# Differential attention of a prompt: score matmuls over 64 rows, the two components by turns, keys in pieces of 256

## The chip, the cores and the metric

The kernel runs on one core of one Trainium2 chip. The metric is the device time of one execution in microseconds (us); before the change the median of three runs is 1026.13 us (1025.02 to 1028.12).

## The reference

One layer of a streaming encoder serves a prompt of 512 tokens and a sample of 64 tokens with 256 cached ones; the width is 1024. The layer is a mixer (half gated delta rule, "GDN", half differential attention), attention to a memory of 256 rows, and a feed-forward net. The change lies in the differential attention. It has 4 heads, each with two components of 64 channels, and the same values for both:

```python
# q, k: (batch, positions, 4 heads, 2 components, 64);  v: (batch, positions, 4 heads, 128)
s = einsum('bqhcd,bkhcd->bhcqk', q, k) * 64 ** -0.5
visible = k_pos[None, :] < ((q_pos // 64 + 1) * 64)[:, None]     # causal by chunks of 64
p = softmax(where(visible, s, -inf))
a = p[:, :, 0] - lam * p[:, :, 1]
o = einsum('bhqk,bkhe->bqhe', a, v)                               # then an RMS norm per head
```

The prompt attends to itself, the sample to its 256 cached keys and its own 64.

## The kernel before

Prompt and sample are one axis of T = 576 tokens, channels on the partitions. Weights are split in a high and a low part (`wh`, `wl`, fp32r), and `project` multiplies each 128 output channels in two halves of the tokens (256 and 320) into banks named `pr`. The program first turns and normalizes the input, projects the inputs of the GDN heads, runs the GDN chunks, and then for each of the four heads `h` calls `diff_project(h)` and `diff_head(h, ...)`. After the heads come the memory keys and values (weights as the moving operand), the output projection, the memory attention and the feed-forward net.

`diff_project` projects queries, keys and values of a head. A head's 128 query channels are component 0 (partitions 0 to 63) and component 1 (64 to 127). They are evacuated into a tile `qz` (two of them, taken by turns by the heads) that has a plane for each component, in which the other component's 64 partitions are zero: GpSimd clears them once, at the start. So a score matmul can take all 128 partitions of the keys (`kdT`, in the profile `u`; the cached keys `ckT` are another `u`) and gets one component's scores.

`diff_head` goes through five tiles of 128 queries: t = 4 (the last 64 prompt queries and the 64 of the sample, of which only the latter are used, against 256 + 64 keys), then t = 0 to 3 with 128, 256, 384 and 512 keys. For each component it writes the scores into a bank, `g0` or `g1` (both `g` in the profile; there is one of each), masks a corner (L976), takes the row's maximum on VectorE (L980), scales it (L981), and lets ScalarE write the exponentials into `p0` or `p1` (L983). The two are combined on VectorE (L985 to L988), turned by TensorE into a bank `ba` (L113, `tr`), copied to `aT`, and multiplied with the values into `gs`. All matmuls go through one helper at L107, so in the profile they are told apart by their tiles. GpSimd also clears the end of a short tile (L990).

The order of the work on each engine is not the order of the code: a scheduler places the instructions by dependency, priority and modelled times, so matmuls of one head's attention stand between those of the next head's projections.

Of the kernel before, what the change touches and what calls it, by code (L numbers as in the profile page):

```python
# [8 lines left out]
F32 = mybir.dt.float32  # L9
# [6 lines left out]
P = 128  # L16
D = 1024
KT = 8
SEQ = 512
DEC = 64  # L20
T = SEQ + DEC
HALVES = ((0, 256), (256, T - 256))
PAST = 256
# [14 lines left out]
def hybrid_layer_kernel(  # L38
# [10 lines left out]
    V, A, G = nc.vector, nc.scalar, nc.gpsimd  # L49
# [17 lines left out]
    cp = ctx.enter_context(tc.tile_pool(name="cp", bufs=1))  # L67
# [11 lines left out]
    def nm(s):  # L79
        uid[0] += 1  # L80
        return f"{s}_{uid[0]}"
# [18 lines left out]
    def bank(tag="ba"):  # L100
        return ps.tile([P, 512], F32, tag=tag, name=nm(tag), bufs=BANKS[tag])
# [4 lines left out]
    def mm(out, lhsT, rhs, start=True, stop=True, pin=False, skip_group_check=False):  # L106
        i = nc.tensor.matmul(out, lhsT, rhs, start=start, stop=stop, skip_group_check=skip_group_check)  # L107
        if pin:
            tc.keep_in_program_order(i)
# [83 lines left out]
    def add_to(dst, b, more):  # L193
        A.copy(dst, more)
        V.tensor_tensor(dst, b, dst, ALU.add)
# [39 lines left out]
    def turn(src, n, q, tag, by=None):  # L235

        b = bank(tag)
        for i in range(4):
            o, f = b[:, i * P : i * P + n], src[:n, (4 * q + i) * P : (4 * q + i + 1) * P]
            if by is None:  # L240
                tr(o, f)
            else:
                mm(o, f, by[:n, :n])
        return b.rearrange("p (i t) -> p i t", i=4)[:, :, :n]
# [230 lines left out]
    with tc.issue_after(behind_keys[1]):  # L475
        ones2, triu2 = const([P, P], "ones2"), const([P, P], "triu2")
        G.memset(ones2, 0.0)
        for i in range(2):
            R = slice(i * DEC, (i + 1) * DEC)
            G.memset(ones2[R, R], 1.0)  # L480
        G.tensor_tensor(triu2, triu, ones2, ALU.mult)
# [12 lines left out]
    for a0, n in HALVES:  # L494
        b = bank("pr")
# [7 lines left out]
    b = bank()  # L503
# [37 lines left out]
    def halves_of(dst, src):  # L541

        for i in range(2):
            R = slice(i * DEC, (i + 1) * DEC)
            V.tensor_copy(dst[R], src[R, 4, i::2])

# [24 lines left out]
    for j in range(3):  # L571
        b = bank()
# [14 lines left out]
    for bi in range(2):  # L587
        scale(mn[:, bi, :], mt[:, bi, :], root(squares(mn[:, bi, :], mt[:, bi, :], P), P), gkv, P)
        for q in range(2):
            src = turn(mn[:, bi, :], P, q, "ba")  # L590
# [178 lines left out]
    def normed(q, nb, parts, out):  # L769

        so, co = tiny([P, nb], "tg"), tiny([P, nb], "tg")
        for R, src in parts:
            A.activation(out[R], src, AF.Square)
        V.tensor_reduce(so, out, AX.X, ALU.add)
# [119 lines left out]
    od, kdT = e3[:, 0], e5[:, 0]  # L894
# [2 lines left out]
    cv2 = view(e3, 1, 4, 4 * P).rearrange("p (i b) n -> p i b n", i=2)  # L897
    ckT, cvv = cv2[:, 0].rearrange("p b (c n) -> p (b c) n", n=PAST), cv2[:, 1]

    qz = [cp.tile([P, 2, T], F32, tag=f"qz{i}", name=f"qz{i}") for i in range(2)]  # L900
    with tc.issue_after(behind_keys[0]), tc.issue_after(behind_keys[1]):
        for q2 in qz:
            G.memset(q2[64:, 0, :], 0.0)
            G.memset(q2[:64, 1, :], 0.0)
        G.memset(vs[64:], 0.0)

    def diff_project(h):
        hs = slice(h * P, (h + 1) * P)
        for kind, base in (("q", 2056), ("k", 2568), ("v", 3080)):
            def evac(b, a0, n, more):  # L910
                ts_ = slice(a0, a0 + n)
                if kind == "q":
                    for c in range(2):
                        R = slice(64 * c, 64 * c + 64)
                        if more is not None:
                            add_to(qz[h % 2][R, c, ts_], b[R], more[R])
                        else:
                            (A.copy if c else V.tensor_copy)(qz[h % 2][R, c, ts_], b[R])
                    return
                d = small("zr", [P, 320])[:, :n] if kind == "v" else kdT[:, h, ts_]  # L920
                if more is not None:
                    add_to(d, b, more)
                else:
                    V.tensor_copy(d, b)
                bt = bank()
                for t in range(2):
                    tr(bt[:, t * P : (t + 1) * P], d[:, t * P : (t + 1) * P])
                if a0:
                    tr(bt[:DEC, 256:384], d[:, 256:])
                src, t2 = bt[:, :256].rearrange("p (t d) -> p t d", t=2), slice(a0 // P, a0 // P + 2)  # L930
                if kind == "v":
                    A.copy(vtm[:, t2, hs], src)
                    if a0:
                        A.copy(vs[:DEC, h, :], bt[:DEC, 256:384])
                else:
                    ko = small("ko", [P, 3, P])
                    A.copy(ko[:, :2], src)
                    nc.sync.dma_start(o_dk_p[0, 0, a0 : a0 + 256, h, :].rearrange("(t p) d -> p t d", p=P), ko[:, :2])
                    if a0:
                        A.copy(ko[:DEC, 2], bt[:DEC, 256:384])  # L940
                        nc.sync.dma_start(o_dk_s[0, 0, :, h, :], ko[:DEC, 2])

            project(weights(w2, base + h * P), xs, evac)
        nc.sync.dma_start(o_dv_p[0, 0, :, h, :].rearrange("(t p) d -> p t d", p=P), vtm[:, :, hs])
        nc.sync.dma_start(o_dv_s[0, 0, :, h, :], vs[:DEC, h, :])
# [11 lines left out]
    def diff_head(h, between):  # L957


        hs = slice(h * P, (h + 1) * P)  # L960
        so, co = tiny([P, 5], "ta"), tiny([P, 5], "ta")
        on = small("an", [P, 5, P])
        for t in (4, 0, 1, 2, 3):
            if t == 1:
                between()
            q0 = QT[t][0]
            nk = q0 + P if t < 4 else PAST + DEC
            nb = (nk + P - 1) // P
            pr = []
            mx, l = tiny([P, 2], "ta"), tiny([P, 2], "ta")  # L970
            for c in range(2):
                b = bank(f"g{c}")
                qq = qz[h % 2][:, c, q0 : q0 + P]
                if t < 4:
                    mm(b[:, :nk], qq, kdT[:, h, :nk])
                    V.memset(b[:64, nk - 64 : nk], -1e30)  # L976
                else:
                    mm(b[:, :PAST], qq, ckT[:, h, :])
                    mm(b[:, PAST:nk], qq, kdT[:, h, SEQ:T])
                V.tensor_reduce(mx[:, c : c + 1], b[:, :nk], AX.X, ALU.max)  # L980
                V.tensor_scalar(mx[:, c : c + 1], mx[:, c : c + 1], -0.125, None, ALU.mult)  # L981
                p = small(f"p{c}", [P, 512])
                A.activation(p[:, :nk], b[:, :nk], AF.Exp, bias=mx[:, c : c + 1], scale=0.125, accum_out=l[:, c : c + 1])  # L983
                pr.append(p)
            V.reciprocal(l, l)  # L985
            V.tensor_tensor(l[:, 1:2], l[:, 1:2], nlam, ALU.mult)
            V.tensor_scalar(pr[1][:, :nk], pr[1][:, :nk], l[:, 1:2], None, ALU.mult)
            V.scalar_tensor_tensor(pr[0][:, :nk], pr[0][:, :nk], l[:, 0:1], pr[1][:, :nk], ALU.mult, ALU.add)  # L988
            if nk < nb * P:
                G.memset(pr[0][:, nk : nb * P], 0.0)  # L990
            bt = bank()
            aT = small("aT", [P, 4, P])
            for kb in range(nb):
                tr(bt[:, kb * P : (kb + 1) * P], pr[0][:, kb * P : (kb + 1) * P])
            A.copy(aT[:, :nb, :], v4(bt, nb))
            po = bank("gs")[:, :P]
            for kb in range(nb):
                if t < 4:
                    vv = vtm[:, kb, hs]
                else:  # L1000
                    vv = cvv[:, kb, hs] if kb < 2 else vs[:, h, :]
                mm(po, aT[:, kb, :], vv, start=kb == 0, stop=kb == nb - 1)
            A.activation(pr[1][:, :P], po, AF.Square, accum_out=so[:, t : t + 1])
            A.copy(on[:, t, :], po)

        def finish():
            V.tensor_scalar(so, so, 1.0 / P, EPS, ALU.mult, ALU.add)
            rpow(co, so)
            V.tensor_tensor(on, on, co.unsqueeze(2).to_broadcast([P, 5, P]), ALU.mult)
            b, b2 = bank(), bank()  # L1010
            for t in range(4):
                tr(b[:, t * P : (t + 1) * P], on[:, t, :])
            tr(b2[:, :P], on[:, 4, :])
            for src, ts_ in ((b, slice(0, SEQ)), (b2[:, DEC:P], slice(SEQ, T))):
                A.activation(od[:, h, ts_], src, AF.Identity, scale=dn)

        return finish
# [23 lines left out]
    for w, out in ((w_mem_k, o_mk), (w_mem_v, o_mv)):  # L1041
        dst = tokens
        for f in range(2):
            fs = slice(512 * f, 512 * f + 512)
            bs = [bank("pr") for _ in range(2)]
            for kc in range(4):
                wt = split_weights(w[0, 256 * kc : 256 * kc + 256, fs], [P, 2, 512])
                for k in (2 * kc, 2 * kc + 1):
                    for t in range(2):
                        ts_ = slice(t * P, (t + 1) * P)  # L1050
# [10 lines left out]
            if out is o_mk:  # L1061
                for i in range(2):
                    b = bank()
# [79 lines left out]
    for k2 in range(KT // 2):  # L1143
        b = bank()
# [6 lines left out]
    for h in range(H):  # L1151
# [15 lines left out]
        for t, (q0, _) in enumerate(QT):  # L1167
            t0, n = TT[t]
            kk, kl = (mkT, mkl) if t < 4 else (cmT, cml)
            b = bank(("gs", "g0", "g1")[t % 3])  # L1170
# [25 lines left out]
        for i in range(2):  # L1196
            b, b2 = bank(("g0", "gs")[i]), bank(("g1", "ba")[i])
# [335 lines left out]
    for m in range(KT):  # L1533
# [3 lines left out]
        if m in (3, 4):  # L1537
            t = m - 3
# [43 lines left out]
```

## Time and profile before

| | |
|---|---|
| median of three runs | 1026.13 us |
| the profiled execution, and its span | 1024.58 us, 1022.9 us |
| granted TensorE clock, mean | 0.995 |
| TensorE matmuls, busy | 1002.1 us (98%) |
| VectorE, ScalarE, GpSimd, busy | 703.3, 535.3, 57.1 us |
| score matmuls (`g<-u,qz`), first to last start | 279.7 to 377.0 us |

The page gives the span in shares by engine and the chain of work that ended last. A row of the group view reads: line, engine, operation, output tile <- input tiles, shape, count, then busy us, mean ns of one, and idle time before. For TensorE a form such as 64*128 is the rows and columns of the array that the instruction uses, and 64x256 the partitions and elements of an operand. A timeline row has start, duration, engine, line, tiles and the number of equal instructions merged. PEld is the load of a matmul's stationary operand, which normally runs under the matmul before. An fp32 matmul appears as two instructions, each with its load; an fp32r matmul as one.

### The profile page before, as it was taken

How to read it: one execution, taken by the hardware profiler on the slowest of the kernel's cores; microseconds unless marked ns; L12 is line 12 of the kernel's file. 1: busy time of each engine (PE TensorE's matmuls, PEld its weight loads, DVE VectorE, ACT ScalarE, POOL GpSimd, SP SyncE). 2: the span in 40 equal slices, each digit the busy share in tenths (PEclk: the TensorE clock that was granted, in tenths of full speed). 3: DMA queues.
4: the chain of work that ended last, by engine and by line, in shares of the span. 5: the costliest groups of instructions: out<-in, count | busy, mean ns of one | idle time of the engine just before them, and what ended most of it. 6: DMA issues, size and time to landing. Idle time of an engine off the chain costs nothing.

```text
span 1022.9 us, 17296 instructions
## 1 busy us (share of the span) xinstructions
PE 1002.1 (98%) x6630; PEld 921.1 (90%) x6630; DVE 703.3 (69%) x1529; ACT 535.3 (52%) x1170; POOL 57.1 (6%) x123
## 2 busy tenths in 40 slices
PE   9999999999999999999999999999999999999996
PEld 7989899998888877899999998999999999999986
DVE  6666785676567676665665886757766677777883
ACT  6654664443364665544454656655545554555434
POOL 3441010100000000000000000000000000000000
PEclk9999999999999999999999999999999999999999
DMA  7432320100312255624121233422222222222202
GB/s 210 124 109 68 103 90 22 44 21 22 104 47 81 74 190 185 186 83 125 44 60 42 64 113 93 125 83 83 83 83 84 83 83 83 83 83 86 80 1 93
DMA packets 121254, 89.99 MB, mean 88 GB/s; under 512 B 5506, under 2 KB 112128, under 8 KB 120660
## 3 DMA queue, kind: packets, MB, share of 16 engines
q1 hardware_dynamic: 120804, 88.24, 29.0%
q8 instruction: 52, 0.85, 0.3%
q10 hardware_dynamic: 368, 0.66, 0.2%
q14 instruction: 30, 0.25, 0.1%
HBM read 79.14 MB, written 9.74 MB: 87 GB/s over the span
## 4 chain that ended last, share of the span: by engine, by line
PE 84%; DVE 3%; issue 3%; ACT 2%; POOL 2%; DMA 1%; POOLq 0%; ACTq 0%; DVEq 0%; SPq 0%
PE pr L107 49%; PE g L107 14%; PE ba L107 10%; PE gs L107 7%; PE ba L113 2%; PE g L113 2%; DMA r<-in_w_ff_dram 1%; DVE wl L162 0%; POOL tg L208 0%; DVE p L457 0%; DMA out_dram<-S 0%; DMA S<-in_state_gdn_dram 0%; POOL X L604 0%; DVE on L780 0%; ACT L645 0%
## 5 line engine op out<-in xcount | busy, mean ns | idle before, releaser
L107 PE MATMUL pr<-u,wh 128*128 128x320 f32 (+2 forms) x1240 | 327.1, 342 | 1.0 <-DVE p L323 1.0
L107 PE MATMUL pr<-u,wl 128*128 128x256 f32 (+1 forms) x816 | 228.3, 304 | 0.0
L107 PEld LDWEIGHTS pr<-u,wh 128*128 128x128 f32 x1240 | 211.5, 188 | 17.1 <-DVE p L323 1.3
L107 PEld LDWEIGHTS pr<-u,wl 128*128 128x128 f32 x816 | 149.8, 189 | 3.5 <-issue 0.7
L162 DVE TENSOR_TENSOR wl<-raw,wh 128x1024 fp32r<-128x1024 f32 x65 | 79.5, 1223 | 43.4 <-ACT wh L161 41.6
L161 ACT CAST wh<-raw 128x1024 fp32r<-128x1024 f32 x65 | 68.2, 1049 | 72.6 <-PE pr L107 55.7
L107 PE MATMUL pr<-u,w2h 128*128 128x320 f32 (+1 forms) x384 | 99.3, 343 | 2.8 <-DVE u L1415 2.8
L1330 ACT CAST w2h<-r 128x512 fp32r<-128x512 f32 x56 | 34.7, 620 | 92.6 <-PE pr L107 89.5
L107 PE MATMUL pr<-f,w2h 128*128 128x320 f32 (+1 forms) x288 | 73.8, 340 | 0.0
L107 PEld LDWEIGHTS pr<-u,w2h 128*128 128x128 f32 x384 | 65.7, 190 | 8.1 <-DVE u L1415 3.1
L107 PE MATMUL pr<-u,w2l 128*128 128x256 f32 (+1 forms) x256 | 65.7, 298 | 0.0
L107 PE MATMUL ba<-u,wl 128*128 128x288 f32 x360 | 54.0, 300 | 2.1 <-ACT keep L1366 2.0
L1415 DVE TENSOR_TENSOR u<-u,pr 128x256 f32<-128x256 f32 x96 | 43.0, 450 | 18.6 <-PE pr L107 18.0
L107 PEld LDWEIGHTS ba<-u,wl 128*128 128x128 f32 x360 | 50.4, 192 | 2.7 <-ACT keep L1366 2.7
L107 PEld LDWEIGHTS pr<-f,w2h 128*128 128x128 f32 x288 | 48.7, 188 | 4.1 <-issue 1.2
L107 PEld LDWEIGHTS pr<-u,w2l 128*128 128x128 f32 x256 | 47.7, 192 | 1.6
L107 PE MATMUL pr<-f,w2l 128*128 128x256 f32 (+1 forms) x192 | 48.8, 295 | 0.0
L1331 DVE TENSOR_TENSOR w2l<-r,w2h 128x512 fp32r<-128x512 f32 x56 | 38.5, 688 | 11.7 <-ACT w2h L1330 11.5
L208 POOL TENSOR_TENSOR tiny<-tiny,nhalf 128x1 f32<-128x1 f32 (+4 forms) x10 | 8.2, 822 | 629.6 <-DVE tiny L1479 537.9
L107 PE MATMUL pr<-wh,u 128*128 128x512 f32 x128 | 41.2, 401 | 0.0
L107 PEld LDWEIGHTS pr<-f,w2l 128*128 128x128 f32 x192 | 35.2, 188 | 1.1
L1375 ACT ACTIVATE c<-c 128x288 f32<-128x288 f32 x48 | 21.0, 442 | 28.6 <-DVE c L1374 28.6
(503 smaller groups left out, 2076.9 us busy)
## 6 DMA issues: line engine op xcount, KB each, us to landing
raw<-in_w_ff_dram SPq DMA_DIRECT2D x36, 512.0 KB
raw<-in_w_in_dram SPq DMA_DIRECT2D x28, 512.0 KB
r<-in_w_ff_dram SPq DMA_DIRECT2D x56, 256.0 KB
raw<-in_w_mem_k_dram SPq DMA_DIRECT2D x8, 512.0 KB
raw<-in_w_mem_v_dram SPq DMA_DIRECT2D x8, 512.0 KB
raw<-in_w_out_dram SPq DMA_DIRECT2D x8, 512.0 KB
raw<-in_w_mem_q_dram SPq DMA_DIRECT2D x8, 512.0 KB
raw<-in_w_mem_o_dram SPq DMA_DIRECT2D x8, 512.0 KB
```

Of the source, the lines that this page charges most:

```text
L107: i = nc.tensor.matmul(out, lhsT, rhs, start=start, stop=stop, skip_group_check=skip_group_check)
L113: i = nc.tensor.transpose(out, in_, ident[:n, :n])
L161: A.copy(wh, raw)
L162: V.tensor_tensor(wl, raw, wh.bitcast(F32), ALU.subtract)
L208: G.tensor_tensor(out, in_, bc(nhalf[: in_.shape[0], 0:1], list(in_.shape)), ALU.pow)
L1330: A.copy(wh, src)
L1331: V.tensor_tensor(wl, src, wh.bitcast(F32), ALU.subtract)
L1375: A.activation(c, c, AF.Relu)
L1415: V.tensor_tensor(am, am, b, ALU.add)
```

## The change

`qz` loses its second plane and its zeros: both components stand in one plane of 128 partitions, evacuated at full height, and the clearing on GpSimd goes. Each score matmul takes 64 partitions of queries and keys, 0 to 63 for component 0 and 64 to 127 for component 1. The keys are cut into pieces of at most 256, and the code issues for each piece first component 0, then component 1. What follows (mask, maximum, exponentials) is unchanged and starts when both components are issued. Per head 12 matmuls become 16.

```diff
--- before.py
+++ after.py
@@ -897,11 +897,8 @@
     cv2 = view(e3, 1, 4, 4 * P).rearrange("p (i b) n -> p i b n", i=2)
     ckT, cvv = cv2[:, 0].rearrange("p b (c n) -> p (b c) n", n=PAST), cv2[:, 1]
 
-    qz = [cp.tile([P, 2, T], F32, tag=f"qz{i}", name=f"qz{i}") for i in range(2)]
+    qz = [cp.tile([P, T], F32, tag=f"qz{i}", name=f"qz{i}") for i in range(2)]
     with tc.issue_after(behind_keys[0]), tc.issue_after(behind_keys[1]):
-        for q2 in qz:
-            G.memset(q2[64:, 0, :], 0.0)
-            G.memset(q2[:64, 1, :], 0.0)
         G.memset(vs[64:], 0.0)
 
     def diff_project(h):
@@ -910,12 +907,10 @@
             def evac(b, a0, n, more):
                 ts_ = slice(a0, a0 + n)
                 if kind == "q":
-                    for c in range(2):
-                        R = slice(64 * c, 64 * c + 64)
-                        if more is not None:
-                            add_to(qz[h % 2][R, c, ts_], b[R], more[R])
-                        else:
-                            (A.copy if c else V.tensor_copy)(qz[h % 2][R, c, ts_], b[R])
+                    if more is not None:
+                        add_to(qz[h % 2][:, ts_], b, more)
+                    else:
+                        V.tensor_copy(qz[h % 2][:, ts_], b)
                     return
                 d = small("zr", [P, 320])[:, :n] if kind == "v" else kdT[:, h, ts_]
                 if more is not None:
@@ -968,15 +963,17 @@
             nb = (nk + P - 1) // P
             pr = []
             mx, l = tiny([P, 2], "ta"), tiny([P, 2], "ta")
-            for c in range(2):
-                b = bank(f"g{c}")
-                qq = qz[h % 2][:, c, q0 : q0 + P]
+            sc = [bank(f"g{c}") for c in range(2)]
+            keys = [(kdT[:, h], k0, min(k0 + 256, nk), 0) for k0 in range(0, nk, 256)]
+            if t == 4:
+                keys = [(ckT[:, h], 0, PAST, 0), (kdT[:, h], PAST, nk, SEQ - PAST)]
+            for src, k0, k1, d in keys:
+                for c in range(2):
+                    R = slice(64 * c, 64 * c + 64)
+                    mm(sc[c][:, k0:k1], qz[h % 2][R, q0 : q0 + P], src[R, k0 + d : k1 + d])
+            for c, b in enumerate(sc):
                 if t < 4:
-                    mm(b[:, :nk], qq, kdT[:, h, :nk])
                     V.memset(b[:64, nk - 64 : nk], -1e30)
-                else:
-                    mm(b[:, :PAST], qq, ckT[:, h, :])
-                    mm(b[:, PAST:nk], qq, kdT[:, h, SEQ:T])
                 V.tensor_reduce(mx[:, c : c + 1], b[:, :nk], AX.X, ALU.max)
                 V.tensor_scalar(mx[:, c : c + 1], mx[:, c : c + 1], -0.125, None, ALU.mult)
                 p = small(f"p{c}", [P, 512])
```

The scheduler's order changes only from the first head's scores on as far as TensorE is concerned. The 64 score matmuls stand in it in 40 runs, each between other matmuls; 33 of the runs hold one component only. Three places on TensorE:

The first head's first prompt tile, 128 keys (`g0` is component 0, `g1` component 1, `pr` a projection). Before the change TensorE has here:

```order
L107 MATMUL pr_643_3450<-u_7_94,wl_642_3447 128x256
L107 MATMUL g0_527_2935<-u_4_78,qz0_2679 128x128
L107 MATMUL pr_643_3450<-u_7_94,wh_641_3446 128x512
L107 MATMUL g1_529_2942<-u_4_78,qz0_2679 128x128
L107 MATMUL pr_643_3450<-u_7_94,wl_642_3447 128x256
L107 MATMUL pr_643_3450<-u_7_94,wh_641_3446 128x512
L107 MATMUL pr_643_3450<-u_7_94,wl_642_3447 128x256 x2
L107 MATMUL pr_643_3450<-u_7_94,wh_641_3446 128x512
```

After it, at the same place of the program:

```order
L107 MATMUL pr_643_3448<-u_7_94,wl_642_3445 128x256
L107 MATMUL g0_527_2928<-u_4_78,qz0_2679 128x128
L107 MATMUL pr_643_3448<-u_7_94,wh_641_3444 128x512
L107 MATMUL pr_643_3448<-u_7_94,wl_642_3445 128x256
L107 MATMUL pr_643_3448<-u_7_94,wh_641_3444 128x512
L107 MATMUL pr_643_3448<-u_7_94,wl_642_3445 128x256 x2
L107 MATMUL pr_643_3448<-u_7_94,wh_641_3444 128x512
L107 MATMUL pr_644_3467<-u_6_93,wh_641_3444 128x320 x2
L107 MATMUL g1_528_2929<-u_4_78,qz0_2679 128x128
```

Before, one projection matmul stands between the two components; after, eight.

The second head's sample tile, 256 cached keys (`u_2_76`) and 64 of its own (`u_4_78`); `ba` is a transpose, `gs` the product with the values. Before the change:

```order
L107 MATMUL pr_651_3529<-u_6_93,wh_646_3500 128x320
L107 MATMUL g0_592_3265<-u_2_76,qz1_2680 128x256
L107 MATMUL gs_551_3017<-u_4_78,aT_550_3012 128x128 x3
L107 MATMUL g0_592_3265<-u_4_78,qz1_2680 128x64
L107 MATMUL g1_594_3272<-u_2_76,qz1_2680 128x256
L107 MATMUL g1_594_3272<-u_4_78,qz1_2680 128x64
L107 MATMUL pr_651_3529<-u_6_93,wh_646_3500 128x320
```

After it, at the same place of the program:

```order
L107 MATMUL g0_592_3259<-u_2_76,qz1_2680 128x256
L113 MATMUL ba_549_3006<-ident_79,p0_547_2995 128x128 x3
L107 MATMUL g0_592_3259<-u_4_78,qz1_2680 128x64
L107 MATMUL pr_651_3524<-u_6_93,wl_647_3496 128x320
L107 MATMUL pr_651_3524<-u_6_93,wh_646_3495 128x320 x2
L107 MATMUL pr_651_3524<-u_6_93,wl_647_3496 128x320
L107 MATMUL gs_551_3012<-u_4_78,aT_550_3007 128x128 x3
L107 MATMUL pr_651_3524<-u_7_94,wh_646_3495 128x320 x2
L107 MATMUL pr_651_3524<-u_7_94,wl_647_3496 128x320
L107 MATMUL pr_651_3524<-u_7_94,wh_646_3495 128x320 x2
L107 MATMUL g1_593_3260<-u_2_76,qz1_2680 128x256
L107 MATMUL g1_593_3260<-u_4_78,qz1_2680 128x64
```

Before, component 0 is cut once by other work and component 1 follows it; after, four score matmuls stand in three runs, no two components side by side.

The second head's tile of 512 keys, before the change:

```order
L107 MATMUL pr_717_3813<-u_7_94,wl_716_3810 128x256
L107 MATMUL g0_630_3400<-u_4_78,qz1_2680 128x512
L113 MATMUL ba_616_3356<-ident_79,p0_613_3343 128x128 x2
L107 MATMUL pr_717_3813<-u_7_94,wl_716_3810 128x256
L107 MATMUL pr_717_3813<-u_7_94,wh_715_3809 128x512
L107 MATMUL pr_718_3834<-u_6_93,wh_715_3809 128x320
L107 MATMUL gs_618_3361<-u_4_78,aT_617_3357 128x128 x2
L107 MATMUL pr_718_3834<-u_6_93,wh_715_3809 128x320
L107 MATMUL g1_632_3407<-u_4_78,qz1_2680 128x512
L107 MATMUL pr_718_3834<-u_6_93,wl_716_3810 128x320
```

After it, at the same place of the program:

```order
L107 MATMUL pr_718_3831<-u_7_94,wl_716_3809 128x320
L107 MATMUL pr_718_3831<-u_7_94,wh_715_3808 128x320 x2
L107 MATMUL g0_630_3396<-u_4_78,qz1_2680 128x256 x2
L107 MATMUL g1_631_3397<-u_4_78,qz1_2680 128x256 x2
L107 MATMUL pr_718_3831<-u_7_94,wl_716_3809 128x320
```

Before, each component is one matmul of 512 in a place of its own; after, two pieces of component 0 are followed by two of component 1, in one run.

## The prediction

> **What bounds it.** I read the page first, then TensorE's waits in the stretch where the four heads run, then the rows of the score matmuls, and last the few places where this kernel already puts matmuls of 64 rows between matmuls of 128.
>
> ```profile
> span 1022.9 us, 17296 instructions
> PE 1002.1 (98%) x6630; PEld 921.1 (90%) x6630; DVE 703.3 (69%) x1529; ACT 535.3 (52%) x1170; POOL 57.1 (6%) x123
> PE 84%; DVE 3%; issue 3%; ACT 2%; POOL 2%; DMA 1%; POOLq 0%; ACTq 0%; DVEq 0%; SPq 0%
> ```
>
> TensorE is busy for 98% of the span and carries 84% of the chain that ended last. A busy row alone is weak evidence, because the ends of pipelined matmuls are modelled, so I look at the stage itself. The score matmuls lie between 279.5 and 377.0 us. The windows view of the stretch around them, and the waits of TensorE from 140 us (where the first queries are evacuated) to 382 us, read:
>
> ```profile
> 276.00:382.00 106.00, 104.91 (x618) 87.33 (x617) 72.68 (x240) 63.28 (x209) 4.54 (x7) 1.00 0.32 102
> PE gs L107 <- DVE on L780: 2.1, 4, 0.9
> PE gs L107 <- DMA S<-in_state_gdn_dram: 0.3, 1, 0.3
> ```
>
> In 106 us the matmul row is busy 104.91, VectorE 72.68 and ScalarE 63.28, and in 242 us TensorE's matmuls waited for anybody only 2.4 us. While a head's softmax runs, the next head's projections fill TensorE. So in this stage time is what TensorE spends: what the change takes from its row comes off the end, what it adds goes on.
>
> **The score matmuls now.** By tile and form they are these (an fp32 matmul is two instructions in the trace, so 48 matmuls are 96 rows):
>
> ```profile
> L107 PE MATMUL g<-u,qz 128*128 128x256 f32 x32 | 9.1, 386 | 0.0
> L107 PE MATMUL g<-u,qz 128*128 128x512 f32 x16 | 8.6, 617 | 0.0
> L107 PE MATMUL g<-u,qz 128*128 128x384 f32 x16 | 6.9, 514 | 0.0
> L107 PE MATMUL g<-u,qz 128*128 128x128 f32 x16 | 3.5, 300 | 0.0
> L107 PE MATMUL g<-u,qz 128*128 128x64 f32 x16 | 2.6, 247 | 0.0
> 294.76 1.06 PE L107 MATMUL g<-u,qz 128*128 128x512 f32 x2
> 295.65 0.38 PE L113 MATMUL ba<-ident,p 128*128 128x128 f32 x2
> ```
>
> The mean durations contain the pipeline's latency; what counts is when the next one starts. Two of 512 columns start at 294.76 and the next work starts at 295.65: 0.89 us, or 0.87 ns per column of one instruction. All 96 stream 32x256 + 16x(512+384+128+64) = 25,600 columns, 22.3 us. That is the most that is at stake: perfect pairing would save half, 11.1 us.
>
> **What removes work.** Half the rows of the old operand were zeros; the new matmuls have 64 rows each but the same number of columns, so alone each holds the array as long as before. Time is saved only where a matmul of rows 0 to 63 and one of rows 64 to 127 stand next to each other, so that both can stream at once. The order shows how often that is. The code issues the components by turns, but the scheduler hands them out by its own priorities: the 64 matmuls stand in 40 separate runs, and only 7 runs hold both halves. An fp32 matmul is two passes, and the second pass of one half can meet only the first pass of the other. Over these 7 runs the meeting passes have 384+256+128+256+128+256+128 = 1,536 columns, 1.3 us at 0.87 ns. Bounds are 0 (they stream one after the other) and -1.3; no run here shows two halves streaming at once and none shows them refusing, the operands and the banks (g0, g1) are disjoint, and I take -1.3.
>
> **What adds work.** Every one of the 40 runs stands between matmuls of 128 rows, and the kernel shows already what such a change of row count costs. One place is a transpose of the 64 sample rows, the other a 64-row block of the triangular inverse. TensorE's timeline in three windows:
>
> ```profile
> 49.13 0.30 PE L107 MATMUL pr<-u,wl 128*128 128x320 f32 x1
> 49.37 0.46 PE L113 MATMUL g<-ident,u 64*128 64x64 f32 x4
> 49.76 0.56 PE L107 MATMUL pr<-u,wh 128*128 128x320 f32 x2
> 50.15 0.31 PE L107 MATMUL pr<-u,wl 128*128 128x320 f32 x1
> 50.29 0.46 PE L107 MATMUL pr<-u,wh 128*128 128x320 f32 x2
> ...
> 170.34 0.38 PE L107 MATMUL g<-Y,X 128*128 128x128 f32 x2
> 170.66 0.68 PE L107 MATMUL g<-X,Y 64*64 64x64 f32 x8
> 171.26 0.94 PE L107 MATMUL g<-Y,X 128*128 128x128 f32 x6
> ...
> 299.01 0.31 PE L107 MATMUL pr<-u,wh 128*128 128x320 f32 x1
> 299.16 0.61 PE L107 MATMUL g<-u,qz 128*128 128x256 f32 x2
> 299.60 0.83 PE L107 MATMUL gs<-u,aT 128*128 128x128 f32 x6
> ```
>
> First place: a 320-column fp32r matmul holds the array 0.14 (50.15 to 50.29), so the one at 49.13 is done streaming at 49.27. The next 128-row pair starts at 49.76 and takes 0.56 where the same pair takes 0.46 at 50.29, so it really streams from 49.86. Of these 0.59 us the four 64-column matmuls need 4x0.055 = 0.22 (eight take 0.22 longer than four: 0.68 against 0.46). The rest, 0.37, is the price of going in and out. Second place: two of 128 columns need 0.22, so they are done at 170.56; eight of 64 need 0.44; the next start at 171.26, and six of them take 0.94 where six take 0.83 at 299.60, so 0.11 more: 171.26 + 0.11 - 170.56 - 0.44 = 0.37. If the 64-column matmuls are paced at 0.06 instead of 0.055, the first reading gives 0.35 and the second 0.33. The third window is the score matmul as it stands now: 299.01 plus 0.14 is 299.15, it starts at 299.16, two of 256 columns take 0.44, which is their 512x0.87 = 0.445; no price at all. Where it comes from is seen in the weight loads:
>
> ```profile
> 48.98 0.19 PEld L107 LDWEIGHTS pr<-u,wl 128*128 128x128 f32 x1
> 49.36 0.32 PEld L113 LDWEIGHTS g<-ident,u 64*128 64x128 f32 x4 [0.19 <-ACT u L283]
> 49.75 0.30 PEld L107 LDWEIGHTS pr<-u,wh 128*128 128x128 f32 x2
> L107 PEld LDWEIGHTS g<-u,qz 128*128 128x128 f32 x96 | 15.6, 189 | 3.3 <-ACT p L983 1.2
> L113 PEld LDWEIGHTS g<-ident,u 64*128 64x128 f32 x12 | 1.0, 138 | 0.5 <-ACT u L283 0.5
> ```
>
> The weights of 49.13 were loaded at 48.98, under the matmul before. The load of the 64-row group starts only at 49.36, 0.09 after the array ran dry, and that of the next 128-row matmul at 49.75, when the group has drained too: on both sides the load is bare. I take 0.35 for a run in and out: 40 x 0.35 = +14.0 us. Bounds: 40 x 0.33 = 13.2 and 40 x 0.37 = 14.8; if a score run waited anyway for a bank or a query, part of its price would be hidden, which the 2.4 us of waits limit.
>
> The Trainium skill, "TensorEngine Tiling (Array Packing)", section Key Properties, says that changing the tiling mode, not just the tile, drains TensorE; the trace agrees, with about 0.09 us before each bare load, and this is the rule that speaks against the change. The Trainium skill, "TensorE: Matmul & The Clock Gate", section LDWEIGHTS, says that a load takes its time by columns whatever its rows; here 64 rows of 128 columns take 138 ns and 128 rows 189 ns, so the trace differs. By the page each way in would be about 0.05 us dearer than my two readings and the sum 2 us higher (an estimate); the measured loads decide.
>
> **The rest.** Keys in pieces of 256 make 128 instructions out of 96. The columns are the same and two of 256 take what one of 512 takes (0.44 against 0.445), so I put them at 0; their weight loads run under the streaming within a run. The query's evacuation becomes full height:
>
> ```profile
> L194 ACT COPY qz<-pr x8: 355/367/367, 148.2 to 327.4; 64x256 f32<-64x256 f32 x8
> L195 DVE TENSOR_TENSOR qz<-pr,qz x8: 398/422/428, 149.2 to 329.0; 64x256 f32<-64x256 f32 x8
> L918 ACT COPY qz<-pr x4: 420/420/422, 158.8 to 338.3; 64x320 f32<-64x320 f32 x4
> L903 POOL MEMSET qz<- x2: 572/574/577, 49.7 to 138.3; 64x576 f32 x2
> L904 POOL MEMSET qz<- x2: 573/573/573, 50.9 to 139.0; 64x576 f32 x2
> ```
>
> Per head one L194 copy (0.37), one L918 copy on ScalarE (0.42) and one L195 addition (0.42) go: 3.2 us of ScalarE and 1.7 of VectorE in all. They free a `pr` bank a little sooner, but TensorE waits there for nothing, so they can't return more than the 2.1 us it waited for VectorE; I take -0.3. The four memsets (2.3 us) go from a GpSimd that is busy 4.54 of 106 us; nobody waits for them: 0. No DMA is moved. The order of VectorE and ScalarE around the scores changes in places, which I can't price by a row; I allow 2 us each way, from the same 2.4 us of waits, and take 0.
>
> **Sum.** +14.0 - 1.3 - 0.3 = +12.4 us. The profiled execution took 1024.58 us, 1.7 more than its span, and would become 1037.0. It was 1.55 us faster than the median of the three runs (1026.13), so on the median's footing the forecast is 1038.5 us, 1.2% slower.
>
> **Rivals.** (1) The pairs stream together and the changes of row count are free where only rows change. Then the order's 1.3 us is gained: 1026.1 - 1.3 - 0.3 = 1024.5, within 0.3%. Against it stand both places above, of which the first also changes rows only, 64*128. Chance 3%. (2) Faster: the array finds the partner half beyond the neighbour in the queue, so that most of the 22.3 us pair up; 11.1 saved, and with free changes 1026.1 - 11.1 - 0.3 = 1014.7. It decides where more than about 10 us of streaming meets a change price under 0.2 us. The Trainium skill, "TensorE: Matmul & The Clock Gate", section Part 3: Packing small matmuls, says that tiles in different row groups run concurrently; no run here shows it, and the order leaves few neighbours for it. With the price of 14.0 paid it would still be +2.6 (1028.7), about at the edge of measurement. Chance 5% for faster, 2% for that edge. (3) The softmax gets late. VectorE already waits for scores:
>
> ```profile
> DVE g L976 <- PE g L107: 8.9, 14, 1.4
> ```
>
> If component 0's first step now stands behind component 1's pieces and TensorE's transposes then wait for the softmax, a piece of 256 in two passes (0.44) on each of the 16 prompt tiles would add 7.0: 1045.5. It needs TensorE to run out of projections, which it hardly does (2.4 us). Chance 7%.
>
> **Chances.** The forecast has 83%, the rivals 3, 7 and 7. Measurement can tell about 0.3% (3 us) from no change. The range goes from 1033 (price 0.30 because waits hide some, 12.0, full overlap, 2.1 back from VectorE, 2 from the order: about +6.6) to 1042 (0.37 each, 14.8, no overlap, 1 from the order: +15.8). Slower by more than 0.3%: 83 + 7 + half of the edge, 0.91; faster 0.05; same 0.04.
>
> **What would show it.** In the changed profile the score matmuls should read 64*128, 128 of them; before each run of them a bare weight load about 0.1 after the array ran dry, and after it a first 128-row matmul about 0.10 longer than its like; TensorE's rows outside the scores unchanged; starts of neighbouring halves less than a pass apart. I am wrong if the runs cost under 0.2 each way in and out together, if runs of one half overlap with something, or if TensorE's waits in 276 to 382 us grow by more than 2 us.

## The result and the profile after

The changed kernel takes 1033.99 us (median of 6 runs, 1032.78 to 1035.71), the kernel before 1026.28 (6 runs): a ratio of 1.0081, 95% interval 1.0067 to 1.0095. It is 7.7 us slower; 1038.5 had been forecast, with a range of 1033 to 1042. The profiled execution took 1034.31 us. Further below, one execution each of the paired kernel and of the kernel without pieces was slow at a lower granted clock (1076.10 and 1077.81 us, clock 0.847) and is left out of the ratios.

The page of the changed kernel, its span, busy times and the chain that ended last:

```profile
span 1032.6 us, 17349 instructions
PE 1011.9 (98%) x6662; PEld 922.5 (89%) x6662; DVE 701.7 (68%) x1525; ACT 532.8 (52%) x1162; POOL 55.0 (5%) x119
PE 84%; DVE 4%; issue 3%; ACT 2%; POOL 2%; DMA 1%; POOLq 0%; ACTq 0%; DVEq 0%; SPq 0%
```

TensorE still carries the chain, its busy row grew by 9.8 us and the span by 9.7; VectorE, ScalarE and GpSimd each lost about 2 us, without use. The views by tile in the changed kernel, of the scores and of a matmul of the memory attention that nothing in the change touches; columns are min/median/max ns, then first to last start:

```profile
L107 PEld LDWEIGHTS g<-u,qz x128: 182/186/187, 279.1 to 393.8; 64*128 64x128 f32 x128
L107 PE MATMUL g<-u,qz x128: 216/376/480, 279.1 to 394.0; 64*128 64x256 f32 x80, 64*128 64x128 f32 x32, 64*128 64x64 f32 x16
L107 PE MATMUL g<-u,ql x24: 274/282/389, 496.2 to 566.1; 128*128 128x256 f32 x24
```

TensorE's waits in the changed kernel from 140 to 400 us:

```profile
PE gs L107 <- DVE on L780: 1.5, 3, 0.9
PE gs L107 <- DMA S<-in_state_gdn_dram: 0.7, 1, 0.7
PE g L107 <- ACT Y L738: 0.2, 1, 0.2
```

The same untouched matmul before:

```profile
L107 PE MATMUL g<-u,ql x24: 278/282/387, 486.9 to 556.7; 128*128 128x256 f32 x24
```

The scores start 0.6 us earlier than before (279.1 against 279.7), and the memory attention 9.3 us later. So all of the loss, about 10 us, lies in the stretch of the heads, and TensorE's waits did not grow (2.4 us; before the change also 2.4, up to 382 us). What happens there is seen in one run of 64-row matmuls, component 0 of the first prompt tile, in TensorE's timeline:

```profile
281.50 0.40 PE L107 MATMUL pr<-u,wh 128*128 128x512 f32 x1
281.73 0.28 PE L107 MATMUL pr<-u,wl 128*128 128x256 f32 x1
281.94 0.48 PE L107 MATMUL g<-u,qz 64*128 64x128 f32 x2
282.36 0.50 PE L107 MATMUL pr<-u,wh 128*128 128x512 f32 x1
```

and in that of its weight loads:

```profile
281.50 0.19 PEld L107 LDWEIGHTS pr<-u,wl 128*128 128x128 f32 x1
281.94 0.29 PEld L107 LDWEIGHTS g<-u,qz 64*128 64x128 f32 x2 [0.25 <-ACT p L980]
282.36 0.19 PEld L107 LDWEIGHTS pr<-u,wh 128*128 128x128 f32 x1
```

The 256-column matmul of 281.73 needs 0.11, so the array is free at 281.84. The load of the score's weights starts at 281.94, 0.10 later, and the load for the projection after it at 282.36. That projection takes 0.50 where its like at 281.50 takes 0.40, so it streams from 282.46. Of these 0.62 us two passes of 128 columns need 0.21; 0.41 is the price of going in and out. The view puts the idle time before this load down to ScalarE, whose step ended at 281.88, so the place alone would not show that the change of rows sets it. The load of the next run waited for nothing that the profile shows:

```profile
283.92 0.29 PEld L107 LDWEIGHTS g<-u,qz 64*128 64x128 f32 x2 [0.19 <-issue]
```

The array is free at 283.83 there, the load starts 0.09 later, and the same working gives 0.40. Of the 40 loads that begin a run, 27 read "issue" like this one.

Worked in this way, with 0.83 ns per column of a pass, for every run of score matmuls: before, 35 runs held the array for 25.4 us, of which 21.3 are streaming; after, 40 runs hold it for 35.6. The difference is 10.2; the stretch lost 9.9 (0.6 and 9.3). The 33 runs with one component have 0.42 each beyond their streaming; before, a run had 0.12.

### The profile page after: what moved, and what is told of

Its sections match the earlier page's. It is cut to its first block, busy times and chain, and to the rows that moved or that the text cites. A ratio compares the mean times of both kernels' runs of the same rounds, so it can differ in the third digit from the quotient of the medians.

```text
span 1032.6 us, 17349 instructions
## 1 busy us (share of the span) xinstructions
PE 1011.9 (98%) x6662; PEld 922.5 (89%) x6662; DVE 701.7 (68%) x1525; ACT 532.8 (52%) x1162; POOL 55.0 (5%) x119
## 4 chain that ended last, share of the span: by engine, by line
PE 84%; DVE 4%; issue 3%; ACT 2%; POOL 2%; DMA 1%; POOLq 0%; ACTq 0%; DVEq 0%; SPq 0%
PE pr L107 49%; PE g L107 14%; PE ba L107 10%; PE gs L107 7%; PE ba L113 2%; PE g L113 2%; DMA r<-in_w_ff_dram 1%; DVE wl L162 0%; DMA out_dram<-S 0%; POOL tg L208 0%; DVE p L457 0%; DMA S<-in_state_gdn_dram 0%; POOL X L604 0%; POOL X L605 0%; DVE on L780 0%
## 5 line engine op out<-in xcount | busy, mean ns | idle before, releaser
L107 PE MATMUL pr<-u,wl 128*128 128x256 f32 (+1 forms) x816 | 225.5, 301 | 0.0
```

## Experiments

Theory S says that going in and out of 64 rows is what made the change slower, and that pairs of components gain. Rival O says that the new order, the pieces and the later softmax did. The "paired" kernel below is the change with its matmuls kept side by side. Each ratio is to executions of the kernel before from the same set; their medians were 1026.28 us with the change, 1025.26 with the first group of experiments (the next four rows), 1025.57 with the rest.

| kernel | time, us | ratio to before (95%) |
|---|---|---|
| the change | 1033.99 | 1.0081 (1.0067 to 1.0095) |
| pieces and turns, 128 rows | 1026.52 | 1.0006 (0.9998 to 1.0015) |
| paired | 1023.06 | 0.9983 (0.9973 to 0.9994) |
| before, 40 extra matmuls of 64 rows | 1044.15 | 1.0189 (1.0175 to 1.0203) |
| before, 40 extra matmuls of 128 rows | 1031.50 | 1.0060 (1.0046 to 1.0074) |
| paired, 128 rows | 1025.87 | 1.0003 (0.9991 to 1.0016) |
| paired, whole keys | 1024.89 | 1.0002 (0.9989 to 1.0015) |
| paired, tiles 4 and 0 in one run | 1023.35 | 0.9977 (0.9964 to 0.9989) |

**Pieces and turns, but 128 rows.** The zero halves and their evacuation are kept; only the loop over the scores is the change's.

```diff
-                    R = slice(64 * c, 64 * c + 64)
-                    mm(sc[c][:, k0:k1], qz[h % 2][R, q0 : q0 + P], src[R, k0 + d : k1 + d])
+                    mm(sc[c][:, k0:k1], qz[h % 2][:, c, q0 : q0 + P], src[:, k0 + d : k1 + d])
```

> The change with its pieces of 256 and its turns, but 128 rows as before (the zero halves and their evacuation kept): nothing switches between 64 and 128 rows and nothing can pair. Theory S (a run of 64-row matmuls costs about 0.41 us for going in and out, and that is what made the change slower): the scores stream their 25,600 columns as before, so the time is that of before within 0.3% (1023 to 1029). Rival O (the new order, pieces and late softmax made it slower): about as slow as the change, 1032 to 1035.

It takes 1026.52 us, as before. Its score matmuls stand in 39 runs, nearly as scattered as in the change, and hold the array for 25.9 us. So neither the order nor the cut nor the later softmax costs what the change lost (by the end of the interval 1.5 us at most, of about 8): rival O falls, and the 64 rows are left.

**The price alone.** In the feed-forward part of the kernel before, 40 matmuls are added, each between two projections, with 64 rows in one kernel and 128 in the other, in the same order:

```diff
+    extra = bank("g0")
     for g in range(1, NG):
...
             project(weights2(w_ff2[0, (g - 1) * 512 : g * 512, :], m * P), (pend,), add_group(g - 1, m), kt=4)
+            if g < 6:
+                with tc.issue_after(latest[0]):
+                    mm(extra[:, :P], ones[:64], ones[:64])     # the other kernel: ones, ones
```

> The kernel before, with 40 extra fp32 matmuls of 64 rows (ones by ones, 128 columns, into a bank that nobody reads) in the feed-forward part, each alone between two projections of 128 rows. Theory S: 40 x (0.22 streaming + 0.41) = +25 us, 1051. If the price of the two short examples in the profile holds (0.35): +23, 1049. Rival O: 0.22 each, +9, 1035.

> The same 40 extra matmuls at the same places with 128 rows. All theories: 40 x 0.22 = +9 us, 1035. So the run with 64 rows should be longer by 16.4 us under theory S with 0.41, by 14 with 0.35, by under 1 under rival O.

They take 1044.15 and 1031.50. The difference is 12.65 us, 0.32 for each; by the ends of the two ratios it is 0.26 to 0.40. That is nearer to the prediction's 0.35 than to the 0.41 of theory S, and far from rival O. The two traces agree: from the first extra matmul to the 37th they run 241.0 and 228.7 us, 0.34 for each of the 36. The times are under their forecasts by 7 and 3.5 us, so part of what is added to TensorE here seems to be taken up elsewhere; where was not followed. In place, the timelines show the whole price. With 64 rows:

```profile
651.66 0.46 PE L109 MATMUL pr<-u,w2h 128*128 128x320 f32 x2
652.04 0.49 PE L109 MATMUL g<-ones 64*128 64x128 f32 x2
652.46 0.50 PE L109 MATMUL pr<-u,w2h 128*128 128x512 f32 x1
652.80 0.28 PE L109 MATMUL pr<-u,w2l 128*128 128x256 f32 x1
652.92 0.39 PE L109 MATMUL pr<-u,w2h 128*128 128x512 f32 x1
```

A like place with 128 rows:

```profile
649.47 0.46 PE L109 MATMUL pr<-u,w2h 128*128 128x320 f32 x2
649.76 0.38 PE L109 MATMUL g<-ones 128*128 128x128 f32 x2
649.90 0.48 PE L109 MATMUL pr<-u,w2h 128*128 128x512 f32 x1
```

With 64 rows: the pair of 651.66 is done at 651.95 (0.145 each), the next streams from 652.46 + 0.11 = 652.57, and 0.62 less 0.22 of streaming is 0.40. With 128 rows: done at 649.76, where the extra one starts; the next streams from 649.90 + 0.09 = 649.99, after 0.23, which is the streaming alone.

**The components kept side by side.** A tile's score matmuls are chained, and the first of them waits for both banks, so the scheduler leaves them together: 20 runs, each component 0, 1, 0, 1.

```diff
+            begin = len(nc.cur_bb.bb.instructions)
+            with in_order(), tc.high_priority():
-            for src, k0, k1, d in keys:
+                for src, k0, k1, d in keys:
...
+            for e in read[0]:     # the exponentials of the tile before, which free the two banks
+                tc.add_manual_dep(nc.cur_bb.bb.instructions[begin], e.name, ...)
+            read[0] = []
```

> The change with the score matmuls of each tile kept side by side: 20 runs instead of 40, each strictly component 0, 1, 0, 1. Theory S with whole pairs (both halves stream at the same time): 20 x 0.41 + 11.1 for half of the 22.3 us of streaming = 19.3 us, against 25.4 that the score runs of before took in its trace: about -6, so 1020 us. Theory S with the prediction's pairing (only the second pass of one meets the first pass of the other): 22.3 - 7.1 + 8.2 = 23.4, about -2, so 1024. Rival O: the softmax of component 0 starts still later, so not faster than the change, 1034 or more.

It takes 1023.06, 0.9983 of before (0.9973 to 0.9994): the same arithmetic as the change, 10 us faster by its order (0.9983 against 1.0081), and a little faster than the kernel before. The gain is nearer to 1024 than to 1020, but not for the reason given there. The trace shows whole pairs. The run of the first head's tile of 384 keys, in the paired kernel's timeline:

```profile
293.00 0.31 PE L107 MATMUL pr<-u,wh 128*128 128x320 f32 x1
293.24 0.92 PE L107 MATMUL g<-u,qz 64*128 64x256 f32 x8
294.09 0.42 PE L107 MATMUL pr<-u,wh 128*128 128x320 f32 x1
```

The same run in the kernel with 128 rows in the same order (the next experiment):

```profile
294.55 1.47 PE L107 MATMUL g<-u,qz 128*128 128x256 f32 x8
295.77 0.39 PE L107 MATMUL pr<-u,wl 128*128 128x320 f32 x1
```

Eight passes of 1,536 columns need 1.28 one after the other. Here the array is free at 293.14 and the next streams from 294.20 (0.42 against 0.31), 1.06 us, price included: 0.64 for half of the columns, 0.42 for the price. The next matmul starts 0.85 after the run does; with 128 rows it starts 1.22 after. All 20 runs hold the array for 21.3 us, 4.1 less than before; without the second component's waits for its bank inside some runs it would be 20 x 0.42 + 10.7 = 19.1. Only about half of the 4.1 arrives at the end. TensorE's waits of the paired kernel show a new one:

```profile
PE gs L107 <- DVE on L780: 2.2, 3, 1.1
PE ba L113 <- DVE p L996: 1.5, 5, 0.4
```

The turning of the probabilities (L113) now waits 1.5 us, in five places, for the last step of their mixing on VectorE (L996); before it waited 1.3 for another step, once, after the heads. This is rival (3) of the prediction, small, and in this kernel, not in the change.

**The same order with 128 rows.**

```diff
-                        mm(sc[c][:, k0:k1], qz[h % 2][R, q0 : q0 + P], src[R, k0 + d : k1 + d])
+                        mm(sc[c][:, k0:k1], qz[h % 2][:, c, q0 : q0 + P], src[:, k0 + d : k1 + d])
```

> The forced order of the paired version (20 runs, components by turns, pieces of 256) with 128 rows and the zero halves: nothing switches and nothing pairs. Theory S (going in and out of 64 rows costs, whole pairs save): longer than the paired version by half of the 21.3 us of streaming less 20 x 0.41, 2.5 us, so 1025.5, as before. If the paired version's gain came from its order alone: as fast as it, 1023. If its order cost something that pairing made good: slower than before, over 1028.

It takes 1025.87, as before and as expected. So the order by itself gains nothing, and TensorE does not wait for the mixing here. The paired kernel is 2.0 us better by the ratios (0 to 4.4 by their ends, so the trace above is the stronger evidence): what pairing saves, half of 21.3, less 20 times the price, which gives (10.7 - 2.0) / 20 = 0.43 a run, with 0.32 to 0.53 by the ends.

**Without pieces.** One matmul of all keys per component; the sample tile keeps its two.

```diff
-            keys = [(kdT[:, h], k0, min(k0 + 256, nk), 0) for k0 in range(0, nk, 256)]
+            keys = [(kdT[:, h], 0, nk, 0)]
```

> The paired version without pieces: one matmul of up to 512 keys per component (the sample tile keeps its two). If each row half takes its own matmuls in its own time, as the trace of the change reads, the cut and the turns don't matter: 1023, as the paired version, and the two components' passes start together. With the prediction's pairing (only neighbouring passes meet) the long tiles lose 4 x 384 columns: +1.3, 1024.4, and the trace shows three steps of a pass where whole pairs show two.

```profile
330.97 0.46 PE L107 MATMUL pr<-u,wh 128*128 128x320 f32 x2
331.36 1.13 PE L107 MATMUL g<-u,qz 64*128 64x512 f32 x4
332.42 0.41 PE L107 MATMUL pr<-u,wl 128*128 128x320 f32 x1
```

Component 0 with its two passes of 512 stands whole ahead of component 1. The array is free at 331.26 and the next streams from 332.42 + 0.10 = 332.52: 1.26 us, less 0.41, is 0.85, two passes of 512. With neighbours alone it would be three, 1.28. So the two halves run each in its own time, and the cut and the turns are not needed for it. The time, 1024.89, does not show a gain: it is nearer to the 1024.4 that was expected with neighbours alone than to 1023, so only the trace decides between the two. In it the memory attention begins at 486.4, 0.5 us earlier than before but 1.1 later than in the paired kernel (485.3), and the turning waits longer for VectorE, 3.2 us in place of 1.7:

```profile
PE ba L113 <- DVE p L996: 2.0, 7, 0.5
PE ba L113 <- DVE g L986: 1.2, 3, 0.5
```

Then one wait for ScalarE's first copy in the feed-forward, 2.0 us before and 2.8 in the paired kernel, is 4.0:

```profile
PE ba L107 <- ACT keep L1374: 4.0, 1, 4.0
```

The row is the only wait of TensorE's matmuls from 590 to 680 us. The edit touches nothing there, and the profiled execution (1027.03) was 2.1 us above the median; why that copy comes later stays open.

**Fewer runs.** The scores of tiles 4 and 0 (320 and 128 keys) stand side by side in the same two banks: 16 runs.

```diff
-            if t == 4:
-                keys = [(ckT[:, h], 0, PAST, 0), (kdT[:, h], PAST, nk, SEQ - PAST)]
+            if t:     # t == 4 issues tile 0's scores too, from column 320 of the banks
+                sc, off, col = [bank(f"g{c}") for c in range(2)], {}, 0
+                for u in (4, 0) if t == 4 else (t,):
...
```

> The paired version with the scores of tiles 4 and 0 (320 + 128 keys) in one run, side by side in the same two banks: 16 runs instead of 20. Theory S: 4 x 0.33 to 0.41 less, 1021.5. Rival O (late softmax): the merged tiles hold both banks longer, so no gain or a loss of about 1, 1023 to 1024.

It takes 1023.35, 0.9977 of before (0.9964 to 0.9989), which the intervals do not tell from the paired kernel. Theory S's 1021.5 is missed; 1023 to 1024 was what rival O expected here. Its runs hold the array for 21.5 us, no less than the 20 runs: merged runs with a wait for a bank inside last up to 1.8 us, others 1.3. The price saved is spent on waiting within the run, and the turning's waits for VectorE grow from 1.7 us to 3.7 (2.9 and 0.8).

## Why the prediction was right, and which terms were off

What bounds: confirmed. TensorE sets the time in this stretch, what was added to its row came out at the end, and its waits did not grow. A pass streams at 0.83 ns a column and not at 0.87, so 21.3 us were at stake and not 22.3.

The price, +14.0: right in kind, and close in size by luck. Two things were off and cancel. In place it is 0.42 a run in the change and 0.40 among the extra matmuls, not 0.35. The likely reason, which no run tests by itself, is the load on the way in: it takes 186 ns for a score's 64 rows as it took 189 for 128, about 0.05 us more than the loads of the two places. The short loads of 138 ns that I had read as a matter of rows belong to transposes (those of the second place, 134 ns, have only 64 columns); a transpose of 128 rows has them too, in the same window as my first place:

```profile
48.76 0.14 PEld L113 LDWEIGHTS g<-ident,u 128*128 128x128 f32 x1
```

The Trainium skill, "TensorE: Matmul & The Clock Gate", section LDWEIGHTS, says that a load goes by columns whatever its rows; the trace of the change agrees (186 against 189), and the sentence of the prediction that the trace differs was a misreading. The other thing: the runs of before were not free, as the one that I had quoted was. They had 0.12 each beyond their streaming, from loads that wait for a bank or a query. The net is 0.42 - 0.12 = 0.30 from the traces, and 0.32 from the extra matmuls: 40 x 0.32 = 12.8, or 10.4 to 16 by the ends of their ratios.

The pairing, -1.3: undersized. The step that failed is that only a neighbouring pass can meet. In a run with both halves each half streams by itself. The change's own trace shows it: in the run at 331.41 us (the second head's tile of 512 keys) the first pass of component 1 starts at 331.71, while the second piece of component 0, which stands ahead of it in the order, starts at 331.94 (the rows do not name the component; the halves are told apart by the spacing of their starts, 331.41, 331.73, 331.94, 332.16 and 331.71, 332.03, 332.25, 332.46). The seven such runs of the change have 0.3 us in sum beyond the streaming of all their passes, where seven prices of 0.42 would be 2.9, so 2.6 were saved. Rival (2)'s mechanism is real within a run, and does not reach across a matmul of 128 rows, as the prediction had it from the order.

The evacuation, -0.3: not settled. The scores start 0.6 us earlier than before (279.1 against 279.7), but the two kernels with 128 rows, which keep the old evacuation, start them at 279.3 and 279.9.

Sum by the measured terms: 12.8 - 2.6 = +10.2, or +9.6 with the 0.6 of the earlier start, whatever caused it, against 9.7 between the two profiled executions and 7.7 between the medians. The profiled execution of before was 1.7 us faster than the median of its six runs and that of the change 0.3 slower than its own; the forecast, made on the median's footing, carries the profile's own difference. The runs don't settle more than the interval, 6.9 to 9.7, so the forecast of +12.4 was 2.7 to 5.5 us too high.

The rivals: (1), a free change of rows, fell by the two kernels with extra matmuls; (3), a late softmax, by the kernel with 128 rows.

## What to carry to other kernels

A matmul of 64 rows saves nothing by itself: it pays only as a run that holds both halves and saves more streaming than the price of going in and out, here 0.4 us, the time of some 500 columns of an fp32 pass. Look in the scheduled order, not in the source, at how many runs there are and whether both halves stand in each; the same arithmetic was 0.8% slower in 40 runs and 0.2% faster in 20. When a load's duration is read for a price, take it from the same kind of matmul: those of transposes are shorter.

## What the runs showed of the hardware

Two row halves are not bound to one order. In the kernel without pieces four passes of 512 columns took the time of two although both of one half stand ahead of the other's. The Trainium skill, "TensorE: Matmul & The Clock Gate", section Part 3: Packing small matmuls, calls matmuls a strict FIFO that overlap in different row groups with starts a few ns apart. The overlap agrees; the strict order does not hold between the halves, by this reading of the change's run at 331.41, where component 1 started 0.23 us ahead of a matmul of component 0 that stands before it. A change between 64 and 128 rows leaves the array empty for about 0.09 to 0.10 us ahead of a bare load, each way (281.84 to 281.94 and 283.83 to 283.92 on the way in), and streaming starts another 0.10 us or so after the load does (282.36 to 282.46 on the way out): together the 0.40 to 0.42, with the granted clock at 1.00 throughout the stretch.
